# The additions of the MLPs' third group of block products to the residual, issued 200 places ahead in the scheduler's order

## The chip, the cores and the metric

The kernel runs as one program on one core of one Trainium2 chip. The metric is the device time of an execution in microseconds (us). Times inside an execution come from the hardware profiler and count from the first instruction.

The engines are named as in the profile: PE is the matrix engine (PEld its weight loads), DVE the vector engine, ACT the scalar engine, SP the queue that issues most loads. Each takes its instructions strictly in the order in which the program gives them to it, and an instruction that waits for another engine holds what stands behind it.

## The reference, cut to what matters

A trunk of two layers over 512 tokens of width 1024. Each layer has a token mixer, a layer norm, a squared-ReLU MLP of hidden width 4096, a second layer norm, and a gate.

```python
h = layer_norm(DEEPNORM_ALPHA * x + mix, ln_g[i, 0], ln_b[i, 0])
h = layer_norm(DEEPNORM_ALPHA * h + sq_relu_mlp(h, mlp_w1[i], mlp_w2[i]), ln_g[i, 1], ln_b[i, 1])
x = h + jax.nn.sigmoid(h @ ple_w_gate[i]) * (p[i] @ ple_w_proj[i])
...
def sq_relu_mlp(h, w1, w2):
    a = jax.nn.relu(h @ w1)
    return (a * a) @ w2
```

The change concerns the second matrix product of the MLP, `(a * a) @ w2`, and its sum with the residual. Both layers have it.

## The kernel before

**Precision.** Every matrix operand is split into a high part (`whi`, a rounded copy made by ACT at L114) and a low part (`wlo`, the rest, a subtraction by DVE at L116). A product is then three matmuls, high by high, high by low, low by high (`mm3`, L120 to L122). The operands that come from HBM are loaded as "units" of 128x1024: SP loads `raw` (L107), ACT makes `whi`, DVE makes `wlo`. There are three `raw` buffers, so a load waits until the split of the unit three before it has read its buffer.

**The MLP in groups.** The hidden width is cut into four groups of 1024. `hidden(g)` computes group g's activations; `half_blocks` (L355 on ACT, L356 to L364 on DVE) splits them in 2x2 blocks and forms sums of blocks. `block_product` multiplies one group with its part of `w2` in seven block products instead of eight (a Strassen scheme). `weight_sums` (L376 loads into `r`, L382 to L388 on DVE) forms the sums of weight blocks that this takes. A group's products run while the next group's activations are computed, in the order that the strings of `PERIODS` spell: T is a stretch of `hidden`, Q a product. The loop's index g is 1 for the first group's products and 3 for the third's, which run beside the activations of the fourth; the fourth group's products (g = 4) run alone, followed by the layer norm.

**A product.** Each has two halves of 128 tokens (c = 0 and 1), 12 matmuls each, into one PSUM bank each. Products named "x" use the two banks `py0` and `py1` and add up there one after another; "y" and "z" use two of the four `pj` banks. After each half, one DVE addition (L462, L466 or L468) adds the bank to the residual `acc`. The next product of the same banks may not write a bank before that addition has read it.

**The end of group 3 and the start of group 4.** Group 3 ends with its products p7 (banks `pj`), p5 (`py`), p4 (the same `pj`) and p3 (`py`), each with a pair of additions at L466. Group 4 has the order p1 (`py`), p7 (`pj`), p6 (`py`), p4, p5, p2, p3. p1 takes two raw units; p7 takes two sums of weights from `r`. Ahead of the fourth group the scheduler also places the gain of the next layer norm, a load into an `a` buffer (L195), which waits until `half_blocks` has read that buffer.

**What sets the order.** The kernel is traced in program order, and a scheduler puts the instructions of all engines in one order by priority, with buffers and banks given out on the way; each engine runs its own part of it. `tc.high_priority(offset=n)` moves what is traced inside n places ahead in that order. Constants: `SOON` is 40, `TURN` is 200, `LEAD` (units) is 100. In `block_product`, the additions of group 4 stood 40 places ahead, those of the groups 1 to 3 at their own place:

```python
with tc.high_priority(offset=SOON if after else 0):
```

Of the kernel before, what the change touches and what calls it, by code (L numbers as in the profile page):

```python
# [28 lines left out]
SOON = 40  # L29
TURN = 200  # L30

PERIODS = ("TTTTTTTT",) + 2 * ("TTQTQTQTQTQTQTQ",) + ("TTTQTQTQTQTQTQQ", "QQQQQQQ")
SUMS = (60, 300, 300, 300)
# [8 lines left out]
def trunk(ctx: ExitStack, tc, a):  # L42
# [21 lines left out]
    def mk(p, shape, tag, dt=F32, **kw):  # L64
        return p.tile(list(shape), dt, tag=tag, name=nm(tag), **kw)

    def f32(t):
        return t.bitcast(F32)
# [21 lines left out]
    def bank(p, tag):  # L90
        return mk(p, [P, T], tag)
# [8 lines left out]
    def behind(ins):  # L100
        return nullcontext() if ins is None else tc.issue_after(ins.ins)

    def unit(src, lead=LEAD):
        n = src.shape[1]
        with tc.high_priority(offset=lead):
            raw = mk(raws, [P, 1024], "raw")
            nc.sync.dma_start(raw[:, :n], src)  # L107
        return split(raw[:, :n], lead)

    def split(f, lead=LEAD):  # L110
        n = f.shape[1]
        with tc.high_priority(offset=lead):
            hi = mk(whip, [P, 1024], "whi", F32R)
            nc.scalar.copy(hi[:, :n], f)  # L114
            lo = mk(wlop, [P, 1024], "wlo", F32R)
            nc.vector.tensor_sub(lo[:, :n], f, f32(hi[:, :n]))  # L116
        return hi, lo

    def mm3(out, sh, sl, mh, ml, start, stop, **kw):
        nc.tensor.matmul(out, sh, mh, start=start, stop=False, **kw)  # L120
        nc.tensor.matmul(out, sh, ml, start=False, stop=False, **kw)  # L121
        marks["pe"] = nc.tensor.matmul(out, sl, mh, start=False, stop=stop, **kw)  # L122
# [36 lines left out]
    with tc.high_priority(offset=FIRST):  # L159
# [7 lines left out]
        for k in range(8):  # L167
            hi, lo = (v[:, k % 4, :] for v in early[k // 4])
            x, w = slots[k][:, 0:T], slots[k][:, T:768]
# [200 lines left out]
    def weight_sums(w, lead):  # L370

        t = [[None, None] for _ in range(4)]

        def load(i, u, src):
            t[i][u] = tmp("r", [P, 1024])
            nc.sync.dma_start(t[i][u], src)  # L376

        with tc.high_priority(offset=lead):
            for u in range(2):
                load(0, u, w[0][1][u])  # L380
                load(2, u, w[1][1][u])
                nc.vector.tensor_sub(t[2][u], t[2][u], t[0][u])  # L382
                load(1, u, w[0][0][u])
                nc.vector.tensor_sub(t[0][u], t[0][u], t[1][u])
                nc.vector.tensor_add(t[1][u], t[2][u], t[1][u])
            for u in range(2):
                load(3, u, w[1][0][u])
                nc.vector.tensor_sub(t[3][u], t[3][u], t[1][u])  # L388
        return t
# [44 lines left out]
            us.append((hi, lo))  # L434
        return us

    def block_product(w, blk, lead, first, after=None, sums=None):

        with behind(marks.pop(("turned", 0), None) if first else None):
            t1, t2, t3, t4 = weight_sums(w, lead)
        seen = set() if first else {(i, j) for i in range(2) for j in range(2)}
        banks = {}

        def product(x, f, name, start, i, j):
            us = [split(v) if f in (t1, t2, t3, t4) else unit(v) for v in f]
            if start:
                banks[name] = [bank(psy, "py%d" % c) if name == "x" else bank(psj, "pj") for c in range(2)]
            t = blk[x]  # L450
            for c in range(2):
                ps = banks[name][c]
                sl = slice(c * P, (c + 1) * P)
                for k in range(4):
                    hi, lo = us[k // 2]
                    ks = slice((k % 2) * 512, (k % 2 + 1) * 512)
                    w_ = hi[:, ks], lo[:, ks]
                    mm3(ps, t[:, 0, k, sl], t[:, 1, k, sl], *w_, start and k == 0, k == 3, skip_group_check=True)
                d = acc[:, 2 - 2 * i + c, j * 512 : (j + 1) * 512]
                with tc.high_priority(offset=SOON if after else 0):  # L460
                    if after and f in (w[1][0], t1, t4, w[1][1]):
                        marks["acc"] = nc.vector.tensor_tensor_reduce(  # L462
                            d, ps, d, 1.0, 0.0, ALU.add, ALU.add, sums[:, 2 - 2 * i + c, j : j + 1]
                        )
                    elif (i, j) in seen:
                        marks["acc"] = nc.vector.tensor_add(d, ps, d)  # L466
                    else:
                        marks["acc"] = nc.vector.scalar_tensor_tensor(d, d, ALPHA, ps, ALU.mult, ALU.add)  # L468
            seen.add((i, j))

        p1 = lambda: product("a11", w[0][0], "x", True, 0, 0)
        p2 = lambda: product("a12", w[1][0], "z", True, 0, 0)
        p6 = lambda: product("s2", t2, "x", False, 1, 0)
        p7 = lambda: product("s3", t3, "y", True, 1, 1)
        p5 = lambda: product("s1", t1, "x", False, 1, 1)
        p4 = lambda: product("a22", t4, "y", False, 1, 0)
        p3 = lambda: product("s4", w[1][1], "x", False, 0, 1)
        for f in (p1, p7, p6, p4, p5, p2, p3) if after else (p1, p2, p6, p7, p5, p4, p3):
            f()
            if after and f is p5:  # L480
                after(0), after(1)
            if after and f is p3:
                after(2), after(3)
            yield

    def mlp_and_gate(layer, h_s, last, turns=()):

        w1, w2 = a[f"w1_{layer}"], a[f"w2_{layer}"]
        blocks = {}
# [45 lines left out]
        for g, period in enumerate(PERIODS):  # L535
            if g < 4:
                tiles = hidden(g)
            if g > 0:
                if g == 4:
                    blk, after, turned, sums, later = norm_blocks(2 * layer + 1)  # L540
                    p_s = (mk(w4, [P, 2, T], "a", F32R), mk(w4, [P, 2, T], "b", F32R))
                    praw = mk(raws, [P, 1024], "raw")
                    nc.sync.dma_start(praw, a[f"pT_{layer}"].rearrange("p k t -> p (k t)"))
                    praw = praw.rearrange("p (k t) -> p k t", k=2)
                    nc.scalar.copy(p_s[0], praw)
                    nc.vector.tensor_sub(p_s[1], praw, f32(p_s[0]))
                w = [[[w2[8 * g - 8 + 4 * i + 2 * j + u] for u in range(2)] for j in range(2)] for i in range(2)]
                products = block_product(w, blocks.pop(g - 1), SUMS[g - 1], g == 1, *((after, sums) if g == 4 else ()))
            for n, op in enumerate(period):
                next(tiles if op == "T" else products)  # L550
                if 0 < g < 4 and (op == "Q" or n == 1):
                    next(ahead, None)
                if g == 4:
                    for _ in ahead:
                        pass
# [125 lines left out]
    first = [bank(psy, "py0"), bank(psy, "py1")]  # L681
# [313 lines left out]
    out_project(a["wso"][12:16], ys[3], False, *after, scale=rms_group(3, bank(psm, "pm")), spread=True)  # L995
    begin("mlp0")
    x_s, late = mlp_and_gate(0, h_s, False, [lambda c=c: after[1](c) for c in (2, 3)])
    begin("hgrn")

# [367 lines left out]
    out_project(a["who"][4:8], halves[1], False, *after)  # L1367
    begin("mlp1")
    mlp_and_gate(1, h_s, True)
    phase[1].__exit__(None, None, None)  # L1370

# [118 lines left out]
```

## Time and profile before

| | |
|---|---|
| median of 3 runs | 1407.03 us (1405.84 to 1407.28) |
| profiled execution | 1406.46 us, its span 1404.7 us |
| PE busy | 1397.1 us (99% of the span) |
| DVE busy | 1078.4 us (77%) |
| ACT busy | 775.8 us (55%) |
| granted TensorE clock | 1.000 |

The profiled execution is 1.8 us longer than its span, which lies ahead of the first instruction and after the last, and 0.6 us under the median of the runs. The groups' additions at L466 are 80 instructions of 0.68 us. A matmul of 512 columns is listed with 0.39 us, but the next one starts 0.227 us later: they overlap, so the distance between starts is what counts for PE.

### The profile page before, as it was taken

Reading aid. Unit: us, or ns where it says so; the run is one execution under the profiler, and the core shown is the slowest. Engines: PE = TensorE matmul, PEld = TensorE weight load, DVE = VectorE, ACT = ScalarE, POOL = GpSimd, SP = SyncE. Lnnn points to the kernel's source line nnn. Section 1 sums busy time; section 2 is a strip of 40 time slices with the busy share of each in tenths; the row PEclk is TensorE's granted clock in tenths of the full one; section 3 lists DMA queues with packets and bytes.
Section 4 is the critical chain, followed back from the end, with each engine's and each line's share of the span. In section 5 each row is a group of like instructions: output and inputs, shape, how many; then the busy total and the mean of one; then the engine's idle time right before and its main releaser. Section 6 shows DMA issues by size and latency. Waiting matters only on the chain.

```text
span 1404.7 us, 20463 instructions
## 1 busy us (share of the span) xinstructions
PE 1397.1 (99%) x7957; PEld 1167.6 (83%) x7957; DVE 1078.4 (77%) x1780; ACT 775.8 (55%) x1165; POOL 2.4 (0%) x11
## 2 busy tenths in 40 slices
PE   9999999999999999999999999999999999999998
PEld 7888888888988888887888888888898888888787
DVE  7998877696867879679885775776785787778886
ACT  7886666573554555455564446465455464544563
POOL 0000000000000000000000000000000000000000
PEclk9999999999999999999999999999999999999999
DMA  8424333323354764653473321222173656646264
GB/s 296 158 99 135 105 106 120 105 91 106 132 183 143 238 219 162 212 194 135 134 288 120 106 91 67 86 94 73 61 255 114 213 177 223 217 151 210 97 243 155
DMA packets 66817, 214.68 MB, mean 153 GB/s; under 512 B 7712, under 2 KB 8352, under 8 KB 66592
## 3 DMA queue, kind: packets, MB, share of 16 engines
q1 hardware_dynamic: 57504, 196.59, 41.1%
q10 hardware_dynamic: 9216, 16.78, 3.3%
q8 instruction: 62, 1.02, 0.3%
q14 instruction: 35, 0.29, 0.1%
HBM read 194.41 MB, written 18.94 MB: 152 GB/s over the span
## 4 chain that ended last, share of the span: by engine, by line
PE 90%; DVE 5%; DMA 2%; ACT 1%; issue 1%; DVEq 0%; ACTq 0%; SPq 0%
PE pj L120 23%; PE pj L122 23%; PE pj L121 23%; PE py L120 5%; PE py L121 5%; PE py L122 5%; DMA r<-in_w 2%; DVE wlo L116 2%; PE py L880 1%; PE py L1147 1%; PE py L882 1%; DVE b L356 1%; DMA raw<-in_w 1%; PE pt L863 0%; DVE acc L466 0%
## 5 line engine op out<-in xcount | busy, mean ns | idle before, releaser
L116 DVE TENSOR_TENSOR wlo<-raw,whi 128x1024 fp32r<-128x1024 f32 x222 | 269.5, 1221 | 170.6 <-ACT whi L114 169.0
L114 ACT CAST whi<-raw 128x1024 fp32r<-128x1024 f32 x222 | 232.7, 1050 | 288.2 <-PE pj L121 147.9
L120 PE MATMUL pj<-b,whi 128*128 128x512 f32 (+1 forms) x1000 | 379.6, 380 | 0.0
L121 PE MATMUL pj<-b,whi 128*128 128x512 f32 (+1 forms) x1000 | 377.3, 377 | 0.0
L122 PE MATMUL pj<-b,wlo 128*128 128x512 f32 (+1 forms) x1000 | 377.3, 377 | 0.0
L122 PEld LDWEIGHTS pj<-b,wlo 128*128 128x128 f32 x1000 | 188.2, 188 | 34.7
L121 PEld LDWEIGHTS pj<-b,whi 128*128 128x128 f32 x1000 | 188.2, 188 | 34.3
L120 PEld LDWEIGHTS pj<-b,whi 128*128 128x128 f32 x1000 | 187.9, 188 | 34.2
L122 PE MATMUL pj<-whi,b 128*128 128x512 f32 x530 | 206.0, 389 | 0.0
L120 PE MATMUL pj<-whi,b 128*128 128x512 f32 x496 | 196.1, 396 | 0.2 <-DVE cv L753 0.2
L121 PE MATMUL pj<-wlo,b 128*128 128x512 f32 x496 | 193.1, 390 | 0.0
L122 PEld LDWEIGHTS pj<-whi,b 128*128 128x128 f32 x530 | 99.5, 188 | 20.7 <-DVE b L1342 0.2
L114 ACT CAST whi<-r 128x1024 fp32r<-128x1024 f32 x64 | 67.2, 1053 | 88.3 <-PE pj L121 67.7
L120 PEld LDWEIGHTS pj<-whi,b 128*128 128x128 f32 x496 | 93.1, 188 | 20.7 <-issue 0.7
L121 PEld LDWEIGHTS pj<-wlo,b 128*128 128x128 f32 x496 | 93.2, 188 | 18.5
L120 PE MATMUL py<-whi,b 128*128 128x512 f32 x256 | 100.5, 393 | 2.2 <-DVE acc L466 2.2
L122 PE MATMUL py<-whi,b 128*128 128x512 f32 x256 | 99.7, 389 | 0.0
L121 PE MATMUL py<-wlo,b 128*128 128x512 f32 x256 | 99.6, 389 | 0.0
L116 DVE TENSOR_TENSOR wlo<-r,whi 128x1024 fp32r<-128x1024 f32 x64 | 77.7, 1219 | 27.6 <-ACT whi L114 26.8
L120 PEld LDWEIGHTS py<-whi,b 128*128 128x128 f32 x256 | 48.1, 188 | 12.8 <-DVE acc L466 3.0
L122 PEld LDWEIGHTS py<-whi,b 128*128 128x128 f32 x256 | 48.0, 188 | 10.1
L121 PEld LDWEIGHTS py<-wlo,b 128*128 128x128 f32 x256 | 48.1, 188 | 9.8
(375 smaller groups left out, 1934.4 us busy)
## 6 DMA issues: line engine op xcount, KB each, us to landing
raw<-in_w SPq DMA_DIRECT2D x112, 512.0 KB, 3.7
r<-in_w SPq DMA_DIRECT2D x64, 512.0 KB, 4.2
raw<-in_wssd SPq DMA_DIRECT2D x38, 512.0 KB, 3.9
a<-csd SPq DMA_DIRECT2D x16, 512.0 KB, 3.7
raw<-in_wso SPq DMA_DIRECT2D x16, 512.0 KB, 3.8
pre<-sg ACTq DMA_DIRECT2D x32, 256.0 KB, 4.8
whi<-pre SPq DMA_DIRECT2D x16, 512.0 KB, 5.4
wlo<-pre SPq DMA_DIRECT2D x16, 512.0 KB, 6.3
```

Of the source, the lines that this page charges most:

```text
L114: nc.scalar.copy(hi[:, :n], f)
L116: nc.vector.tensor_sub(lo[:, :n], f, f32(hi[:, :n]))
L120: nc.tensor.matmul(out, sh, mh, start=start, stop=False, **kw)
L121: nc.tensor.matmul(out, sh, ml, start=False, stop=False, **kw)
L122: marks["pe"] = nc.tensor.matmul(out, sl, mh, start=False, stop=stop, **kw)
L356: nc.vector.tensor_sub(lo, f, f32(hi))
L880: nc.tensor.matmul(yd[64 * r : 64 * r + 64, sl], xdt[:, c, r, :], m[:, r, sl], start=True, stop=c == 0)
L882: nc.tensor.matmul(yd[64 * r : 64 * r + 64, sl], pv[:, c - 1, r, :], ecs[:, r, (c - 1) * P : c * P], start=False, stop=True,)
L1147: nc.tensor.matmul(ps[r][32 * b : 32 * b + 32, base + n * c : base + n * c + n], kk[r][:, ts], moving(r, 4 * c + b), start=True, stop=True,)
```

## The change

`block_product` gets an argument `soon`, the offset for its additions. The call for g = 3 gives it TURN = 200, in both layers. Groups 1, 2 and 4 keep theirs.

```diff
-    def block_product(w, blk, lead, first, after=None, sums=None):
+    def block_product(w, blk, lead, first, after=None, sums=None, soon=0):
...
-                with tc.high_priority(offset=SOON if after else 0):
+                with tc.high_priority(offset=SOON if after else soon):
...
-                products = block_product(w, blocks.pop(g - 1), SUMS[g - 1], g == 1, *((after, sums) if g == 4 else ()))
+                products = block_product(w, blocks.pop(g - 1), SUMS[g - 1], g == 1, *((after, sums) if g == 4 else ()), soon=TURN if g == 3 else 0)
```

No instruction is added or removed. DVE, ACT, PE and SP each get the same instructions in another order near the end of group 3, in the same way in both layers; below is layer 0. A name ends in a number of its own: `py_850` and `py_851` are the banks of group 3's products p5 and p3, `pj_5343` and `pj_5344` those of its p7 and p4; `py_934` and `py_935` are those of group 4's p1, `pj_5650` and `pj_5651` those of its p7. `raw_5602` and `raw_5608` are p1's two units, `raw_5531` is the second unit of group 3's p3.

DVE, while PE computes group 3's p5 and the last activations; + is the order now, - the order before:

```order
 L356 TENSOR_TENSOR b_815_4952<-a_5225,b_815_4952 128x512
+L466 TENSOR_TENSOR acc_94<-py_850_5096,acc_94 128x512
 L388 TENSOR_TENSOR r_5596<-r_5596,r_5583 128x1024
-L466 TENSOR_TENSOR acc_94<-py_850_5096,acc_94 128x512
 L388 TENSOR_TENSOR r_5599<-r_5599,r_5592 128x1024
+L466 TENSOR_TENSOR acc_94<-py_851_5097,acc_94 128x512
+L356 TENSOR_TENSOR b_819_4956<-a_4959,b_819_4956 128x512
 L116 TENSOR_TENSOR wlo_5535<-raw_5531,whi_5533 128x1024
-L356 TENSOR_TENSOR b_819_4956<-a_4959,b_819_4956 128x512
 L116 TENSOR_TENSOR wlo_5606<-raw_5602,whi_5604 128x1024
-L466 TENSOR_TENSOR acc_94<-py_851_5097,acc_94 128x512
```

The additions of p5 stand earlier; the split of `raw_5531`, which frees a `raw` buffer, now stands behind the second of them and behind an L356 that it used to precede.

DVE, some five rows later, at the end of group 3:

```order
+L466 TENSOR_TENSOR acc_94<-pj_5344,acc_94 128x512
+L116 TENSOR_TENSOR wlo_5644<-r_5580,whi_5642 128x1024
+L116 TENSOR_TENSOR wlo_5648<-r_5589,whi_5646 128x1024
+L466 TENSOR_TENSOR acc_94<-py_850_5096,acc_94 128x512
 L360 TENSOR_TENSOR b_5373<-a_5225,b_5373 128x2x256
-L116 TENSOR_TENSOR wlo_5644<-r_5580,whi_5642 128x1024
 L362 TENSOR_TENSOR a_5225<-a_5225 128x2x256
-L116 TENSOR_TENSOR wlo_5648<-r_5589,whi_5646 128x1024
+L116 TENSOR_TENSOR wlo_5680<-r_5583,whi_5678 128x1024
+L356 TENSOR_TENSOR blk_4958<-b_5027,blk_4958 128x512
+L466 TENSOR_TENSOR acc_94<-py_851_5097,acc_94 128x512
```

The last three additions of group 3 (p4's second half and both of p3's) used to stand behind the whole of `half_blocks`' sums; now they stand among them, p3's second one behind four other operations. The five rows ahead of this piece, the same in both, are an L356, the split of `raw_5608` (L116), p4's first addition (L466) and two L356.

PE at the same place, before:

```order
L121 MATMUL py_851_5097<-wlo_5535,blk_4315 128x512
L122 MATMUL py_851_5097<-whi_5533,blk_4315 128x512
L120 MATMUL pj_5650<-whi_5642,blk_4957 128x512
L121 MATMUL pj_5650<-wlo_5644,blk_4957 128x512
L122 MATMUL pj_5650<-whi_5642,blk_4957 128x512
```

PE at the same place, now:

```order
L121 MATMUL py_851_5097<-wlo_5535,blk_4315 128x512
L122 MATMUL py_851_5097<-whi_5533,blk_4315 128x512
L120 MATMUL py_934_5614<-whi_5604,b_815_4952 128x512
L121 MATMUL py_934_5614<-wlo_5606,b_815_4952 128x512
L122 MATMUL py_934_5614<-whi_5604,b_815_4952 128x512
```

Before, group 3's p3 was followed by 23 of p7's 24 matmuls, then by p1; now p1, which writes the banks that p3 has just left, follows p3 directly, and p7 comes after it.

SP at the same place:

```order
 L376 DMA r_5599<-in_w_0 128x1024
 L107 DMA raw_5602<-in_w_0 128x1024
+L195 DMA a_5563<-in_ln 128x1024
 L107 DMA raw_5608<-in_w_0 128x1024
-L195 DMA a_5563<-in_ln 128x1024
 L107 DMA raw_5808<-in_w_0 128x1024
```

The load of the norm's gain now stands ahead of the load of p1's second unit. On ACT, the casts of the same stretch change places in step with DVE's rows.

## Prediction

> **What bounds the kernel now.** I read the page first (busy times, the chain that ended last, the costly groups), then PE's waits, then the stretch around each wait in order of time.
>
> ```profile
> PE 1397.1 (99%) x7957; PEld 1167.6 (83%) x7957; DVE 1078.4 (77%) x1780; ACT 775.8 (55%) x1165; POOL 2.4 (0%) x11
> PE 90%; DVE 5%; DMA 2%; ACT 1%; issue 1%; DVEq 0%; ACTq 0%; SPq 0%
> L120 PE MATMUL py<-whi,b 128*128 128x512 f32 x256 | 100.5, 393 | 2.2 <-DVE acc L466 2.2
> ```
>
> PE works through 99% of the span, so time is won only where PE stands still or by taking matmuls away, and the change takes none away. The 77% of DVE is a mean and says nothing on the ends of stages. The last row shows the one place in the MLPs where PE waits: 2.2 us on the additions that this change moves. PE's waits say the same:
>
> ```profile
> PE py L120 <- DVE acc L466: 2.2, 2, 1.1
> PE pm L155 <- DVE y L152: 1.1, 1, 1.1
> PE pj L120 <- DVE cv L753: 0.2, 1, 0.2
> ```
>
> Two waits, one a layer, are most of what all of PE's waits come to. PE in order of time shows what they are:
>
> ```profile
> 658.02 0.39 PE L120 MATMUL pj<-whi,blk 128*128 128x512 f32 x1
> ...
> 663.01 0.39 PE L121 MATMUL pj<-wlo,blk 128*128 128x512 f32 x1
> 664.46 0.50 PE L120 MATMUL py<-whi,b 128*128 128x512 f32 x1 [1.06 <-DVE acc L466]
> 664.80 0.40 PE L121 MATMUL py<-wlo,b 128*128 128x512 f32 x1
> ...
> 1314.70 0.50 PE L120 MATMUL py<-whi,b 128*128 128x512 f32 x1 [1.14 <-DVE acc L466]
> 1315.04 0.40 PE L121 MATMUL py<-wlo,b 128*128 128x512 f32 x1
> ```
>
> Starts are 0.227 us apart when nothing waits (22 steps from 658.02 to 663.01). From 663.01 the next should have started at 663.24; it started at 664.46, so 1.22 us are lost, and 0.11 us more since the first matmul after a wait takes 0.34 us to the second. In layer 1 the idle time is 0.08 us longer (1.14 against 1.06). Lost are 1.33 + 1.41 = 2.74 us: that is 0.19% of 1407 and the most that removed waits can bring. The first matmul that waits is p1 of group 4; it may write the bank only when group 3's p3 has been added. Why DVE is late:
>
> ```profile
> 642.21 1.23 DVE L388 TENSOR_TENSOR r<-r,r 128x1024 f32<-128x1024 f32 x1
> 643.35 1.22 DVE L116 TENSOR_TENSOR wlo<-raw,whi 128x1024 fp32r<-128x1024 f32 x1
> 644.49 0.69 DVE L356 TENSOR_TENSOR b<-a,b 128x512 fp32r<-128x512 f32 x1
> ...
> 649.71 1.23 DVE L116 TENSOR_TENSOR wlo<-raw,whi 128x1024 fp32r<-128x1024 f32 x1 [2.20 <-ACT whi L114]
> 650.85 0.68 DVE L466 TENSOR_TENSOR acc<-pj,acc 128x512 f32<-128x512 f32 x1
> 651.95 1.29 DVE L356 TENSOR_TENSOR b<-b,b 128x512 fp32r<-128x512 f32 x2 [0.42 <-ACT b L355]
> ...
> 661.98 0.68 DVE L466 TENSOR_TENSOR acc<-pj,acc 128x512 f32<-128x512 f32 x1
> 662.59 1.22 DVE L116 TENSOR_TENSOR wlo<-r,whi 128x1024 fp32r<-128x1024 f32 x1
> 663.72 1.28 DVE L466 TENSOR_TENSOR acc<-py,acc 128x512 f32<-128x512 f32 x2
> ```
>
> DVE stands still for 2.20 us until 649.71, waiting for the cast of p1's second unit, and then works without a pause worth the name until p3's additions at 663.72. An operation on 128x1024 holds DVE for 1.14 us (643.35 to 644.49), one on 128x512 for 0.60 us. The cast itself waited for a load, and that load for a buffer; the chain of work shows it in both layers:
>
> ```profile
> 644.60 3.93 DMA raw<-in_w
> 648.62 1.05 ACT whi L114
> ...
> 1287.71 5.00 DMA r<-in_w
> ...
> 1295.19 3.58 DMA raw<-in_w
> 1298.87 1.05 ACT whi L114
> ```
>
> The load was issued at 644.60, as the split that started at 643.35 ended (it reads the buffer), and took 3.93 us.
>
> **The change, part by part.** *Added and removed instructions:* none, 0 us. *The additions ahead of p3's:* PE waits for none of them before, and earlier ones release banks earlier: 0 for PE. They cost DVE its place, counted next.
>
> *DVE up to the load.* Before the split that frees the buffer, DVE now has done p7's second addition (0.60 us; it now stands ahead of the split that releases a buffer for the last `r` loads, so these and the second L388 come that much later, L388 at 642.81), then p5's second addition and the L356 that stood behind the split (1.20 us). The split starts at 642.81 + 1.14 + 1.20 = 645.15 and not 643.35: the load of p1's second unit is issued 1.80 us later, at 646.40. What hid that before, DVE's 2.20 us of idle time, is the time in which this load runs, so nothing hides it: the split of the unit, 5.11 us after the issue (644.60 to 649.71), starts at 651.51, if the load takes as long as before.
>
> *DVE from there to p3's additions.* In the order given above: split 1.14, p4's addition 0.60, two L356 1.20, p4's second addition 0.60, two splits 2.28. The L355 that the two L356 wait for follow the cast directly now, since ACT has done L523 and L525 ahead of it, so the wait of 0.42 us goes. Sum 5.82: p3's first addition starts at 657.33, and ends 0.68 us later at 658.01. Then its own slot and L360, L362 (1.80), a split 1.14, an L356 0.60: p3's second addition starts at 660.87 and ends at 661.55.
>
> *PE.* p1 now stands where p7's first matmul stood, at 658.02. Until a matmul starts, 0.06 us pass after the addition's end (663.72 + 0.68 = 664.40 to 664.46). So p1's first half waits some 0.05 us. Its second half is due 12 x 0.227 = 2.72 us later, at 660.74, and starts at 661.61: a wait of 0.87 us, 0.98 with the restart. The 5.2 us of p7 that covered p3's additions before lie behind p1 now, and the two effects nearly cancel: 1.33 lost becomes 0.98, a gain of 0.35 us a layer. Layer 1 has the same orders and a wait of the same kind; I take 0.35 there too. Together -0.70 us.
>
> *p7, p6 and what follows on PE.* p7 starts at about 664.5 instead of 658.0; its operands (the splits of its `r` units, right ahead of p3's first addition, and an L356 on `blk` two rows behind the second, which ends at 660.87 + 0.60 + 0.60 + 0.68 = 662.75) are ready 1.7 us ahead, and a late load moves both sides alike. p6 starts after 48 matmuls, at the same place as before. 0 us. *ACT:* casts of the same units in another order, covered by its 45% of idle time; on the way to the end only the one counted.
>
> *SP.* The norm's gain is loaded ahead of the unit, and not behind it:
>
> ```profile
> 637.68 0.33 SPq L376 DMA_DIRECT2D r<-in_w  x1
> 645.20 0.33 SPq L195 DMA_DIRECT2D a<-in_ln  x1
> 667.89 0.33 SPq L107 DMA_DIRECT2D raw<-in_w  x1
> ```
>
> The first of two `r` loads that end in DVE's L388, as the chain has it, L388 itself, and the time from issue to landing of the four L195:
>
> ```profile
> 636.59 3.68 DMA r<-in_w
> ...
> 640.36 1.23 DVE L388 TENSOR_TENSOR r<-r,r 128x1024 f32<-128x1024 f32 x1 [0.38 <-DMA r<-in_w]
> ...
> DMA to landing us min/median/max: 3.7/4.1/5.8
> ```
>
> The gain's load (L195) waits for the L356 that started at 644.49, so it is issued as that ends. This L356 now stands just ahead of the split that frees the `raw` buffer. So the unit's load is issued one split, 1.14 us, behind another load of 512 KB. No row of before has this pair in this order. Bounds: it may cost nothing (the load takes 3.93 and 3.58 us in the two layers, as before), or the unit may take as long as the slowest L195, 5.8 us, which was issued 0.60 us behind the unit's load (644.60 to 645.20). The nearest rows are two `r` loads 1.09 us apart: the first, from 636.59, took 3.68 us; DVE, which waits for both at L388, started 4.53 us after the second was issued (637.68 to 642.21), some 4.44 us of it the load (the first had 0.09 us from landing, 640.27, to DVE's start at 640.36). Layer 1's second load of that pair took 5.00 us. I take 4.44 for both layers: 0.51 and 0.86 us later, and each passes to PE undiminished, since p1 has nothing to spare: +1.37 us. The ends are 0 and (5.8 - 3.93) + (5.8 - 3.58) = 4.09 us.
>
> A later unit's load (667.89) waits for L546 on DVE, which ran at 666.65 and now stands further back:
>
> ```profile
> 666.65 1.22 DVE L546 TENSOR_TENSOR b<-raw,a 128x1024 fp32r<-128x1024 f32 x1
> 680.02 1.05 ACT L114 CAST whi<-raw 128x1024 fp32r<-128x1024 f32 x1 [3.02 <-PE pj L122]
> ```
>
> From p3's second addition at 660.87 there are ten operations of 0.60 and five of 1.14 us ahead of L546, which so starts at 672.6, 5.9 us later. The load then is issued at 673.8 and lands, at 4.4 us, by 678.2; its cast did not start before 680.02, held by PE. 0 us, with 1.8 us of cover.
>
> The Trainium skill speaks against so high a price for the unit's load: DMA: Bandwidth & Descriptors, "Anatomy of one DMA", gives a fit (measured on the GpSimd path) of about 2.0 us fixed plus the bytes at 436 GB/s. By it 512 KB move in 1.2 us, a load 1.14 us behind another would be held by some 0.06 us, and the sum would be -0.6 us. The rows above, 3.68 against 4.44 us, do not agree with it.
>
> *Sum:* -0.70 + 1.37 = +0.67 us. The profiled execution of 1406.46 us becomes 1407.1; from the median of the runs, 0.57 us higher, 1407.7.
>
> **The rivals.**
>
> *1. The load is hardly delayed.* That is the lower end of the SP term. For it: the L195 load is issued while no other load is in flight. Against it: the `r` rows. -0.70 us: 1406.3. The fit that the Trainium skill gives in DMA: Bandwidth & Descriptors would bring this case about.
>
> *2. The waits go altogether*: DVE reaches p3's additions 0.9 us earlier than my sum. For it: most slots come from back-to-back rows, and a faster landing by that much would do it. Against it: the load is issued 1.80 us later for certain if DVE's order holds. -2.74 us: 1404.3.
>
> *3. Slower: p1 waits for its second unit's load in earnest.* One mechanism: the unit's load, now second in the queue, lands late; ACT and DVE stand behind it in order, and every us of it arrives at PE, which no longer has p7 in front as cover. If it takes 5.8 us in both layers the sum is -0.70 + 4.09 = +3.39: 1410.4. It decides (0.2%, 2.8 us) when the two loads together are 3.5 us later than before. For it: that 5.8 was seen in this very stretch; against: with fewer loads ahead of it than L195 had then.
>
> **How the numbers follow.** 0.2% or 2.8 us is about what a measurement of this kernel can tell from no change. The forecast (the wait changes its place and the load is somewhat late, between -0.1 and +2.5 us) gets 0.55, rival 1 gets 0.25, rival 2 gets 0.07, rival 3 gets 0.10, anything else 0.03. Rivals 1 and 2 stay inside 0.2% by their own numbers (2.74 is 0.195%); noise may carry rival 2 over it, so faster gets 0.03, slower 0.10, same 0.87. The range leaves out rival 2's end and most of rival 3: from 1405.2 (rival 1 less a spread of the runs of about 1 us) to 1409.6 (the forecast with both loads 1 us later still).
>
> **What would show it.** After the change PE should still wait for L466, in each layer at both halves of p1: at the first by what the load is late, 0.5 to 0.9 us, and 12 matmuls later at the second by 0.8 to 0.9 us. p1's second unit should be issued about 1.8 us later against PE's place than now, 1.14 us behind L195, and take about 4.4 us. PE's busy time and its clock stay. A wait at the second half alone speaks for rival 1, none at either for rival 2, one of 1.8 us or more at the first half for rival 3. The prediction is wrong if PE waits elsewhere in the two stretches, at p7 above all, or if p1's second unit is issued where it was, which would mean that DVE's rows ahead of it wait less than I count.

## The result, and the profile after

| | median | lowest to highest | against before (95% interval) |
|---|---|---|---|
| before | 1406.11 us | 1405.56 to 1407.28 | |
| after | 1410.94 us | 1410.43 to 1412.26 | 1.0034 [1.0022, 1.0046] |

The change makes the kernel slower, by 4.8 us. The prediction was 1407.7 us, within 1405.2 to 1409.6: it is wrong. The profiled execution of after took 1412.26 us, its span 1410.5 us; that is 5.8 us over the profiled execution of before, and it was the slowest of the runs shown.

The row of the page, and two of PE's waits, that answer to those of before:

```profile
L120 PE MATMUL py<-whi,b 128*128 128x512 f32 x256 | 101.2, 395 | 6.1 <-DVE acc L466 6.1
```

```profile
PE py L120 <- DVE acc L466: 6.1, 3, 3.0
...
PE py L120 <- ACT whi L174: 0.4, 1, 0.4
```

The wait on the additions is where it was expected, but has 6.1 us and not 2.2; no other wait came up in the two stretches. PE in order of time, p3's last matmul and p1's first ones, in layer 0 and then in layer 1:

```profile
658.22 0.39 PE L122 MATMUL py<-whi,blk 128*128 128x512 f32 x1
661.63 0.76 PE L120 MATMUL py<-whi,b 128*128 128x512 f32 x1 [3.03 <-DVE acc L466]
662.20 0.63 PE L121 MATMUL py<-wlo,b 128*128 128x512 f32 x1
...
664.64 0.40 PE L121 MATMUL py<-wlo,b 128*128 128x512 f32 x1
...
1311.63 0.39 PE L122 MATMUL py<-whi,blk 128*128 128x512 f32 x1
1314.49 0.47 PE L120 MATMUL py<-whi,b 128*128 128x512 f32 x1 [2.47 <-DVE acc L466]
...
1318.07 0.50 PE L120 MATMUL py<-whi,b 128*128 128x512 f32 x1 [0.57 <-DVE acc L466]
```

In layer 0 p1 was due 0.227 us after 658.22, at 658.45, and started at 661.63: 3.18 us are lost. Then seven steps, to 664.64, take 3.01 us instead of 1.59: 1.42 us more, because the clock is lowered. The same stretch by windows (the number after POOL is the granted clock):

```profile
661.00:662.50 1.50, 0.87 (x2) 0.80 (x3) 1.47 (x3) 0.38 (x1) 0.00 (x0) 0.52 0.00 0
662.50:664.50 2.00, 2.00 (x6) 1.52 (x6) 2.00 (x4) 2.00 (x4) 0.00 (x0) 0.50 0.00 0
```

The lowered clock did not cost all of these 1.42 us. p1's second half started at 665.78. At the full clock it would have been due at about 664.5, but p3's second addition (664.47, in the next fence) lets it start only 0.68 + 0.06 us later, at 665.21, and with the 0.11 us of a restart that is some 0.5 us sooner than it came. So the clock's own share is about 0.5 us, an estimate from these rows; the rest of the 1.42 us took the place of the wait at the second half, which layer 1 shows.

In layer 1 p1 was due at 1311.86 and started at 1314.49, 2.63 us lost; its second half started 3.58 us after its first instead of 2.72, 0.86 us lost. The clock stayed. Together 4.60 + 3.49 = 8.1 us against 2.74 before: 5.4 of the 5.8 us. The wait at L174 (0.4 us, at the start of the program) is most of the rest.

Why the additions are late: DVE in the stretch before them. The load of p1's second unit, as the chain of work has it (time, duration), stands in the second fence.

```profile
644.66 1.23 DVE L388 TENSOR_TENSOR r<-r,r 128x1024 f32<-128x1024 f32 x1 [0.70 <-DMA r<-in_w]
...
647.00 2.35 DVE L116 TENSOR_TENSOR wlo<-raw,whi 128x1024 fp32r<-128x1024 f32 x2
...
654.99 1.22 DVE L116 TENSOR_TENSOR wlo<-raw,whi 128x1024 fp32r<-128x1024 f32 x1 [5.03 <-ACT whi L114]
...
660.80 0.68 DVE L466 TENSOR_TENSOR acc<-py,acc 128x512 f32<-128x512 f32 x1
...
664.47 0.68 DVE L466 TENSOR_TENSOR acc<-py,acc 128x512 f32<-128x512 f32 x1
```

```profile
648.25 5.58 DMA raw<-in_w
...
1301.61 5.08 DMA raw<-in_w
```

PE reached the end of p3 at 658.45 here and at 658.02 before, so 0.43 us are taken off a difference of times below ("against PE"). L388's second instance then is 2.45 - 0.43 = 2.02 us later than before; p1's second unit is issued 3.65 - 0.43 = 3.22 us later (648.25 against 644.60), its load takes 1.65 us longer (5.58 against 3.93; 1.50 in layer 1), and its split starts 5.28 - 0.43 = 4.85 us later. DVE waits 5.03 us for it, not 2.20. From that split on the order is as I counted it: p3's first addition 5.81 us behind the split (predicted 5.82), its second 3.67 us behind the first (predicted 3.54).

In layer 1 the same steps give less: L388 starts 1298.02 - 1292.80 = 5.22 us later than before, 3.68 of which PE is later too (1311.86 against 1308.18), so 1.54 us against PE.

So the question is what made L388 2.02 us late, when I had counted 0.60. Further up, DVE shows it; the stretch that the section on the change prints begins behind these rows, and the order of DVE differs from before here already. Before, at a split and at the next operation that waits for a load:

```profile
620.13 1.22 DVE L116 TENSOR_TENSOR wlo<-raw,whi 128x1024 fp32r<-128x1024 f32 x1
...
629.55 1.23 DVE L382 TENSOR_TENSOR r<-r,r 128x1024 f32<-128x1024 f32 x1 [1.88 <-DMA r<-in_w]
```

SP's issue of the load that this split allows, in before, and the `r` load behind it, from the chain of before (its time, its length):

```profile
621.38 0.33 SPq L107 DMA_DIRECT2D raw<-in_w  x1
```

```profile
624.31 5.16 DMA r<-in_w
```

After, DVE and SP at the same places:

```profile
618.17 0.69 DVE L466 TENSOR_TENSOR acc<-py,acc 128x512 f32<-128x512 f32 x1
...
621.16 0.68 DVE L466 TENSOR_TENSOR acc<-py,acc 128x512 f32<-128x512 f32 x1
621.76 0.68 DVE L356 TENSOR_TENSOR b<-b,b 128x512 fp32r<-128x512 f32 x1
622.36 1.22 DVE L116 TENSOR_TENSOR wlo<-raw,whi 128x1024 fp32r<-128x1024 f32 x1
...
631.84 1.23 DVE L382 TENSOR_TENSOR r<-r,r 128x1024 f32<-128x1024 f32 x1 [2.42 <-DMA r<-in_w]
```

```profile
623.64 0.33 SPq L107 DMA_DIRECT2D raw<-in_w  x1
625.35 3.10 SPq L376 DMA_DIRECT2D r<-in_w  x2
```

The two additions of p6 (618.17 and 621.16) and an L356 now stand ahead of this split. It frees the `raw` buffer for the second unit of p3, some 20 us ahead of the stretch that I had studied. That unit's load is issued 2.26 - 0.43 = 1.83 us later against PE, so the `r` load follows it by 1.71 us and no longer by 2.93. The `r` load itself is issued 1.04 - 0.43 = 0.61 us later against PE, and now takes 6.4 us from issue to landing; DVE's L382, which waits for it, starts 2.29 - 0.43 = 1.86 us later against PE.

DVE's next split is held by something else as well. ACT's cast for it waits until a store of gate weights (L423, issued by ACT's queue) has landed, and the chain of after runs over these stores in both layers, not over the `r` load. ACT's cast and DVE's split in before:

```profile
630.20 1.05 ACT L114 CAST whi<-raw 128x1024 fp32r<-128x1024 f32 x1 [2.20 <-DMA pre<-whi]
```

```profile
631.30 1.21 DVE L116 TENSOR_TENSOR wlo<-raw,whi 128x1024 fp32r<-128x1024 f32 x1
```

The store, cast and split in after, and the store in layer 1, from the chain:

```profile
626.06 0.33 ACTq L423 DMA_DIRECT2D pre<-whi  x1
...
632.03 1.05 ACT L114 CAST whi<-raw 128x1024 fp32r<-128x1024 f32 x1 [3.61 <-DMA pre<-wlo]
```

```profile
633.11 1.23 DVE L116 TENSOR_TENSOR wlo<-raw,whi 128x1024 fp32r<-128x1024 f32 x1
```

```profile
1279.48 5.73 DMA pre<-whi
```

The view names `pre<-wlo`, but that store lands only at 632.9; the one of `whi` lands at 631.96, 0.07 us ahead of the cast. The two stores are issued where they were against PE (625.64 and 627.00 before, 626.06 and 627.41 now), but take 5.9 and 5.5 us to land, where it was 4.5 and 3.8. Either wait alone would have held the split until about 633 (L382 at 631.84 and its 1.14 us; the cast at 632.03 and its 1.05 us). The split is 1.81 - 0.43 = 1.38 us later against PE. Behind it stands p7's second addition, whose 0.60 us I had counted: 1.38 + 0.60 = 1.98 of L388's 2.02 us. So some 1.4 us, the part that I had not counted, come from one load and two stores that land late together.

### The profile page after: what moved, and what is told of

Read it like the earlier page. It is cut to its first block, busy times and chain, and to the rows that moved or that the text cites. A ratio compares the mean times of both kernels' runs of the same rounds, so it can differ in the third digit from the quotient of the medians.

```text
span 1410.5 us, 20463 instructions
## 1 busy us (share of the span) xinstructions
PE 1398.6 (99%) x7957; PEld 1168.7 (83%) x7957; DVE 1078.7 (76%) x1780; ACT 775.1 (55%) x1165; POOL 2.4 (0%) x11
## 4 chain that ended last, share of the span: by engine, by line
PE 93%; DVE 3%; DMA 3%; ACT 1%; issue 1%; SPq 0%; ACTq 0%; DVEq 0%
PE pj L120 24%; PE pj L121 23%; PE pj L122 23%; PE py L120 5%; PE py L121 5%; PE py L122 5%; DVE wlo L116 1%; PE py L880 1%; PE py L1147 1%; DMA raw<-in_w 1%; PE py L882 1%; DMA r<-in_w 1%; PE pt L863 0%; DMA acc<-in_xw 0%; DVE acc L466 0%
## 5 line engine op out<-in xcount | busy, mean ns | idle before, releaser
L116 DVE TENSOR_TENSOR wlo<-raw,whi 128x1024 fp32r<-128x1024 f32 x222 | 269.6, 1222 | 176.1 <-ACT whi L114 174.9
L116 DVE TENSOR_TENSOR wlo<-r,whi 128x1024 fp32r<-128x1024 f32 x64 | 77.5, 1220 | 25.6 <-ACT whi L114 24.8
```

## The experiments

Theories at the start. A: DVE's rows ahead of splits make the loads late, p1's second unit above all. B: PE has lost its cover, since p1 follows p3 directly and p7 comes behind it. C: the gain's load (L195) ahead of the unit's makes that load slow. All edits are against after.

**p3's additions alone ahead.**

```diff
-                with tc.high_priority(offset=SOON if after else soon):
+                with tc.high_priority(offset=SOON if after else soon if f is w[1][1] else 0):
```

> Only the additions of group 3's last product p3 stand 200 places ahead; those of its other six products keep the place that they had before the change. PE's order is that of the changed kernel (p1 right behind p3), SP's order is that of before. Theory A (the loss comes from additions ahead of DVE's splits, which free the load buffers, so that p1's second unit lands late): the unit's load is issued where it was before, PE waits at neither half of p1, and 2.3 to 2.7 us are won against before (about 1403.6 us). Theory B (the loss comes from PE's order: p7's 23 matmuls no longer cover p3's additions): PE still waits 2 to 3 us a layer at p1 and the time is 1409 to 1411 us. Theory C (the loss comes from the norm's gain loaded ahead of the unit): no loss here either, since SP's order is the old one; the run doesn't tell A from C.

Measured: 1404.67 us, ratio 0.9987 [0.9978, 0.9996]. PE waits for no L466 at all; the longest row of its waits, 1.1 us on L152 at the start of the program, is one that before has too. That is 1.7 us less than its own runs of before (1406.38), not the 2.3 to 2.7 expected. SP's loads and DVE's splits up to p1's second unit have the order of before here, while p1 follows p3 directly on PE as in after. DVE's two additions of p3 and the PE rows that they release (p1's two halves):

```profile
656.81 0.69 DVE L466 TENSOR_TENSOR acc<-py,acc 128x512 f32<-128x512 f32 x1
659.21 0.69 DVE L466 TENSOR_TENSOR acc<-py,acc 128x512 f32<-128x512 f32 x1
```

```profile
658.14 0.39 PE L120 MATMUL py<-whi,b 128*128 128x512 f32 x1
...
660.86 0.39 PE L120 MATMUL py<-whi,b 128*128 128x512 f32 x1
```

Each addition ends about 0.6 to 1.0 us ahead of its matmul (656.81 + 0.69 and 658.14; 659.21 + 0.69 and 660.86). The place of p1 on PE alone costs nothing: B falls as a cause by itself. This version is faster than both kernels.

**The others ahead, p4's and p3's at their old place.**

```diff
+                with tc.high_priority(offset=SOON if after else 0 if f is w[1][1] or f is t4 else soon):
```

> The reverse of the first: the additions of p1, p2, p6, p7 and p5 of group 3 stand 200 places ahead, those of p4 and p3 keep their old place. SP has the changed kernel's order (the gain's load ahead of p1's second unit). Theory A: the unit lands 4 to 5 us late as in the changed kernel, DVE reaches p3's additions that much later, with all of the sums of the activations' blocks still ahead of them, and PE waits 5 to 6 us a layer: 1413 to 1418 us. Theory B (lost cover alone): no loss, 1405 to 1407 us. Theory C: between, 1408 to 1411 us, with the unit's load issued where it was and only its landing late.

Measured: 1418.21 us, ratio 1.0084 [1.0070, 1.0098], the slowest of all, although p7 stands ahead of p1 on PE as before:

```profile
PE py L120 <- DVE acc L466: 7.3, 2, 3.7
```

p7 is not a clean cover here: its own matmuls wait 2.4 us in the two layers for blocks that ACT and DVE make (L355, L356). The clock falls at both waits too (last section). The additions of p1, p2, p6, p7 and p5, for which PE never waited, together do the harm, and p3's do the good; which of the five pairs it is, this run doesn't tell.

**The norm's parameters loaded at its first chunk.** The gain and bias leave this stretch; nothing is computed otherwise.

```diff
-        gb = ln_params(i)
+        gb = []
...
         def chunk(c):
+            gb or gb.extend(ln_params(i))
```

> The changed kernel with the norm's gain and bias loaded only when the first chunk is normalised, so no other load stands right ahead of p1's second unit. Theory A with the price that the trace gives (the unit's load takes 5.6 and 5.1 us behind the gain's, against 3.9 and 3.6 before): the load is issued as late as in the changed kernel but takes 3.6 to 4 us, PE's wait shrinks by 1.5 us a layer, the clock is not lowered in layer 0, and 4 to 5 us of the 4.8 come back: 1406 to 1408 us. Theory C (the gain's load is all of the loss): 1404.5 us or less, with no wait left. Theory B: as slow as the changed kernel, 1410 to 1411 us.

Measured: 1407.69 us, ratio 1.0008 [0.9998, 1.0017]. Beside the 1406.38 us of its own runs of before that is +1.3: 3.5 of the 4.8 us come back. The chain of this run has the unit's load at 3.71 and 3.79 us, as fast as before the change, in place of 5.58 and 5.08:

```profile
647.50 3.71 DMA raw<-in_w
...
1298.30 3.79 DMA raw<-in_w
```

PE still waits on L466, four times and 3.1 us in all:

```profile
PE py L120 <- DVE acc L466: 3.1, 4, 0.9
```

C is real as a part: 5.58 - 3.71 and 5.08 - 3.79 make 3.2 us for both layers, and with the 0.5 us of the clock they come near the 3.5 us. As the whole loss C falls, since PE still waits. The 4 to 5 us that theory A expected back did not come.

**Small stores.** The last eight stores of transformed weights in each layer (L416, L423) write 16 columns of 512, and the loads that read them read another block; so part of the weights is not the reference's.

```diff
-                            nc.scalar.dma_start(to, x)
+                            nc.scalar.dma_start(to[:, : 512 if (u, h) != (1, 1) else 16], x[:, : 512 if (u, h) != (1, 1) else 16])
```

(L416 likewise.)

> The changed kernel in which the last eight stores of prepared gate weights in each layer (ACT's queue, 256 KB each, in the stretch of group 3) store 16 columns of 512; the gate then takes its second half of weights from the first half's stores, so the output is not the reference's. Theory A with loads colliding with stores: the weight load behind DVE's first late L382 takes 5 us or less (6.4 in the changed kernel, 5.2 before), ACT's cast of the unit behind those stores starts 1.4 us earlier, so everything down to p1's second unit comes 1.4 us earlier: PE waits 1.3 to 1.8 us a layer instead of 2.5 to 3.1, the clock stays, and the time is 1406 to 1408 us. If the stores don't matter (the lateness is all DVE's own order): 1410 to 1411 us.

Measured: 1408.75 us, ratio 1.0014 [1.0005, 1.0023], a little above what was expected: +2.4 us against its own runs of before, so 2.4 of the 4.8 come back. The `r` load takes 3.8 us in this run, 6.4 in after, and DVE's L382 finds it landed (no wait is listed):

```profile
628.87 1.22 DVE L382 TENSOR_TENSOR r<-r,r 128x1024 f32<-128x1024 f32 x1
```

ACT's queue issues such stores beside that load, in after the one at 626.06 shown above. So the traffic of the stores is part of what makes the late loads slow. The run changes two things at once, though: the cast that waits for these stores is free earlier too (it starts at 628.92 and waits 0.32 us), so it doesn't tell the `r` load's share from the cast's. The profiled execution was the fastest of its runs, so its waits on L466 (1.9 us in all) are those of a faster run than the median; where the rest of the median's time lies isn't settled.

**p6's additions alone ahead.** By now the rows further up were read, and A was split: A1 holds p6's additions to be the missing part, A2 p5's and the gain's load alone.

```diff
+                with tc.high_priority(offset=SOON if after else soon if f is t2 else 0):
```

> Of group 3's additions only p6's two are issued 200 places ahead; PE and SP have the order of before, DVE differs from before in some ten rows some 25 us ahead of the end of group 3. Upstream theory (A1: p6's additions ahead of the split that frees p3's second raw buffer make that load some 1.8 us late, it then runs together with an r load and two stores, and the whole of DVE up to p1's second unit is some 2 us late): p1's second unit is issued 1.5 to 2.0 us later against PE than before, DVE reaches p3's additions as much later, and since PE has used up p7 as cover before, its two waits of 1.1 us grow to 2.6 to 3.1 us each: 1409.0 to 1410.5 us. Rival (A2: the lateness comes only from p5's additions right ahead of the split and from the gain's load ahead of the unit, p6's additions change nothing that matters): waits as before, 1405.6 to 1406.9 us.

Measured: 1410.51 us, ratio 1.0032 [1.0019, 1.0044]. Two additions some 40 us ahead of p1, for which PE does not wait, make a loss of 4.1 us by themselves, 0.7 us less than the whole change. The profiled execution is the fastest of the five, 1409.22 us, 2.8 us over that of before, and its clock is 1.000; two slower ones, 1412.15 and 1412.45 us, have mean clocks of 0.999 and 0.997. PE and SP have the order of before, and the two waits of before have grown from 1.06 and 1.14 us:

```profile
665.68 0.50 PE L120 MATMUL py<-whi,b 128*128 128x512 f32 x1 [2.61 <-DVE acc L466]
...
1317.54 0.50 PE L120 MATMUL py<-whi,b 128*128 128x512 f32 x1 [2.69 <-DVE acc L466]
```

The upstream rows are those of after again: on SP the load of p3's second unit (622.96) 1.70 us ahead of the `r` load (624.66), which takes 6.3 us, and ACT's two stores, which take 4.9 to 5.8 us. p1's second unit is issued at 646.05 in the chain of this run and lands in 3.70 us, as it did before; only its issue is late, by 1.8 us:

```profile
646.05 3.70 DMA raw<-in_w
```

**All but p6's.**

```diff
+                with tc.high_priority(offset=SOON if after else soon if f is not t2 else 0):
```

> The change without p6's two additions; PE and SP keep the order of the changed kernel, and DVE the same rows ahead of the split that frees the buffer. Upstream theory (A1): p3's second raw unit and the r loads come as in before, p1's second unit is issued 1.2 to 1.8 us later against PE than before instead of 3.2, the wait at p1's first half falls from 3.0 and 2.5 us to 1.0 to 1.7, no lowered clock: 1406.8 to 1408.6 us. Rival (A2): waits and time stay those of the changed kernel, 1410 to 1411.5 us.

Measured: 1407.15 us, ratio 1.0008 [0.9999, 1.0017], 0.7 us over before, which the interval doesn't tell from no change. The wait at p1's second half is there in both layers and that at its first half in one, 2.0 us in all; at the first half 1.0 to 1.7 us in each layer had been expected, and 0 and 0.8 came. The chain has the slow load behind L195 in layer 1:

```profile
1295.25 5.48 DMA raw<-in_w
```

```profile
PE py L120 <- DVE acc L466: 2.0, 3, 0.8
```

A1 holds, A2 falls: without p6's additions most of the loss is gone, with the gain's load still ahead of the unit. But one step of A1 does not hold. On SP the `r` load is as close behind the load of p3's second unit here as in after:

```profile
621.94 0.33 SPq L107 DMA_DIRECT2D raw<-in_w  x1
623.67 4.05 SPq L376 DMA_DIRECT2D r<-in_w  x2
```

It lands in 4.3 us all the same, and the two stores of ACT in 2.6 to 3.2 us. They are issued 1.81 and 3.03 us behind the `r` load here (625.48 and 626.70), 0.71 and 2.06 us behind it in after. So the nearness of the two loads is not by itself what makes the `r` load slow. That p6's additions move it against the stores fits all these runs, and the run with small stores above, but no run moves this distance alone.

**The change, with p7 ahead of p1 in group 4.**

```diff
-        for f in (p1, p7, p6, p4, p5, p2, p3) if after else (p1, p2, p6, p7, p5, p4, p3):
+        for f in (p7, p1, p6, p4, p5, p2, p3) if after else (p1, p2, p6, p7, p5, p4, p3):
```

> The change, and group 4 takes p7 ahead of p1, so that PE has p7's 24 matmuls (5.4 us) between p3 and p1 again, with DVE's additions in the changed order. Theory A (p1's second unit and the additions behind it are late by some 3.2 us, and nothing else is wrong): the cover hides most of it, the waits on L466 sum to under 2 us, no lowered clock: 1404.5 to 1407.0 us. Rival B2 (the split that brings p7's operands stands behind the late unit as well, so p7 waits instead of p1): waits of over 2 us in each layer at p7's first matmuls or at p1, 1409 us or more.

Measured: 1404.19 us, ratio 0.9984 [0.9975, 0.9993], faster than both kernels and about as fast as p3's additions alone, with no wait on L466 left. The time is 0.3 us under what theory A expected, and the cover is not the only reason. p3's second unit is loaded as late as in after (623.37, with p3's end on PE at 658.17, against 623.64 and 658.45); the `r` load behind it takes 5.0 us, not 6.4, and p1's second unit is split at 654.40. DVE in this run:

```profile
647.03 1.22 DVE L116 TENSOR_TENSOR wlo<-r,whi 128x1024 fp32r<-128x1024 f32 x1
...
648.76 1.22 DVE L116 TENSOR_TENSOR wlo<-r,whi 128x1024 fp32r<-128x1024 f32 x1
...
654.40 1.22 DVE L116 TENSOR_TENSOR wlo<-raw,whi 128x1024 fp32r<-128x1024 f32 x1
...
656.14 0.69 DVE L466 TENSOR_TENSOR acc<-py,acc 128x512 f32<-128x512 f32 x1
...
658.54 0.69 DVE L466 TENSOR_TENSOR acc<-py,acc 128x512 f32<-128x512 f32 x1
```

Against PE's end of p3 the unit lands 1.8 us earlier than in after (issued at 647.14, 4.6 us), but its split starts only 0.3 us earlier. DVE no longer stands still in front of it. It does the splits of p7's operands (647.03 and 648.76), L356's and an addition of p4 there, which in after stood behind the late unit (its two splits of `r` at 658.54). So p3's first addition comes 1.7 us behind the unit's split and not 5.8. The second ends at 659.23, and p1's second half, if p1 followed p3 directly on PE, would be due at 658.17 + 2.72 = 660.89: by these rows no wait would be left in layer 0 even without p7 in front, and none either if the split came 0.3 us later, as in after. That is worked out, not run: no run has this order of DVE with p1 directly behind p3. B2 falls, since PE waits nowhere for p7. What made the late unit so dear in after is the ready work that stood behind it on DVE.

The lateness in layer 0, from the traces: the issue of p1's second unit against PE, later than before, and its time from issue to landing:

| kernel | median us | unit issued later | lands in |
|---|---|---|---|
| before | 1406.11 | 0 | 3.93 |
| after | 1410.94 | 3.2 | 5.58 |
| p3 alone | 1404.67 | -0.2 | 3.60 |
| p6 alone | 1410.51 | 1.8 | 3.70 |
| all but p6 | 1407.15 | 0.9 | 4.77 |

The 1.8 and the 0.9 us come to 2.7 of the 3.2.

## Why the prediction was wrong, step by step

- **The additions ahead of p3's "cost DVE its place, counted next": the step that failed.** I counted p7's second addition and p5's, and left out p6's two, which stand ahead of a split too. I had followed the order only from p7's additions on, not at every split that frees a buffer. The term of 0.60 us for L388 measured 2.02 in layer 0 and 1.54 in layer 1: p7's 0.60 was right, and what p6's rows set off, a load and two stores that land late, came on top. The sum had no term for that, nor for ACT's cast, which waits for the stores. p6 alone costs 4.1 us (1410.51 against the 1406.42 of its own runs of before); the change without it costs 0.7 us, and my sum, which had no p6, was +0.67. That these meet is partly chance: there the unit is issued 0.9 us late in layer 0, not 1.8, as its `r` load landed faster than before (4.3 us against 5.2), and its own load then takes longer than I had it (4.77 and 5.48 against 4.44).
- **What was missing in the sum, in us:** L388 1.42 and 0.94, the unit's load 1.14 and 0.64, the clock about 0.5. Together 4.6, and with the forecast's +0.67 that is 5.3; the rows of PE gave 5.4.
- **p5's addition and the L356, 1.20 us:** right, 3.22 - 2.02 = 1.20.
- **The load behind L195, 4.44 us:** too small; 5.58 and 5.08 in after, 4.77 and 5.48 without p6's additions. Against before, after's are 1.65 and 1.50 us more, and not 0.51 and 0.86. Inside the ends I gave (up to 5.8 us), but I took the row of the two `r` loads, which was too fast a neighbour. The fit from the Trainium skill (DMA: Bandwidth & Descriptors, "Anatomy of one DMA"), by which I estimated that a load 1.14 us behind another would be held by some 0.06 us, does not describe these loads, which SP issues: they were held by 1.65 and 1.50 us.
- **DVE from the split to p3's additions, 5.82 us, and the second half's wait, 0.87 us:** right; 5.81 us in layer 0 and, for the wait, 0.86 us in layer 1. In layer 0 the lowered clock filled the time of that wait.
- **p7, the later unit and all else at 0 us:** right; no further wait came. That the lost cover of p7 is made up by earlier additions was right as well: with p3's additions alone ahead PE had neither the cover nor a wait.
- **"PE's clock stays":** wrong in layer 0 of the profiled execution, 1.42 us on the first half and about 0.5 us in the end. It was no accident of that execution: the mean clock is 0.998 in five of the seven of after, the profiled one among them, and 0.999 in the other two, where the profiled execution of before has 1.000 and the runs of before beside the experiments 1.000 or 0.999.
- **Rival 3** gave the right sign and, at 1410.4 us, nearly the right time, and its mark (a wait of 1.8 us or more at p1's first half) came. Its mechanism holds for one part: with the gain's load moved away 3.5 us came back, and p6's additions alone cost 4.1. These two are not parts of one sum, since the second was measured with before's order of PE. That the time came so near is partly luck: the two loads were 3.2 us later than before, not 4.09, and the late L388, which rival 3 did not have, made up the rest.
- **The ends of the range** are each about 0.1 us off their own working: 1406.3 less 1 is 1405.3, and 1407.7 plus 2 is 1409.7. The result lies beyond both values of the upper end.

## What to carry to other kernels

An instruction moved ahead on an in-order engine is paid by whatever stood there: list every row that it passes, back to where it now stands, and mark the rows that free a buffer for a load, since the transfers that moved here met others and landed later still. Move only what somebody waits for: of the two pairs of additions that were moved alone, p3's paid and p6's cost. Where an operation must wait for a late load, look at what stands behind it on its engine: a unit issued 2.4 us late (647.14, p3's end at 658.17) cost nothing once the ready splits and additions stood ahead of it.

## What the hardware showed beyond that

**The clock.** In layer 0 of after the granted clock fell to 0.5 in an idle time of PE of 3.03 us, for about 3.4 us: by the windows shown, 0.52 from 661.00 to 662.50 and 0.50 to 664.50. After idle times of 2.47, 2.61 and 2.69 us, in the rows above, it stayed: in layer 1 of after p1's first half took no longer than its 2.72 us and the wait behind it, and the execution with p6's additions alone has a mean clock of 1.000. That is no bound either: in another execution of that same kernel, 1412.45 us, the mean clock is 0.997, and waits and clock inside it are not recorded. In the second experiment it fell with both waits of 3.7 us:

```profile
670.30:673.70 3.40, 3.40 (x10) 2.66 (x9) 2.58 (x4) 0.00 (x0) 0.00 (x0) 0.50 0.00 0
...
1325.00:1326.20 1.20, 0.00 (x0) 0.00 (x0) 1.20 (x3) 0.00 (x0) 0.00 (x0) 0.77 0.00 0
1326.20:1332.40 6.20, 6.14 (x14) 4.79 (x15) 4.08 (x7) 0.00 (x0) 0.00 (x0) 0.50 0.26 82
```

In layer 0 PE was at work again from 669.47, and the lowered stretch of 3.4 us lies behind that; in layer 1 it began inside the wait (none of PE's work in the window at 0.77) and lasted over 6 us. The Trainium skill's TensorE: Matmul & The Clock Gate ("What's actually happening") describes a window of some 3.4 us that runs on its own; these lengths and the shifting begin agree with it. Its rule of no idle gaps over some 3.4 us ("HAM oscillation — how this bites in real kernels") is not a safe bound here: 3.03 us were enough.

**Transfers in company.** p1's second unit, 512 KB, landed in 3.6 to 3.9 us without the gain's load ahead of it and in 4.5 to 5.6 us when issued 1.14 us behind it. For the `r` load the store behind it goes with its time better than the load ahead of it (layer 0):

| kernel | load ahead by | first store behind by | `r` load lands in |
|---|---|---|---|
| all but p6 | 1.73 | 1.81 | 4.3 |
| before | 2.93 | 1.33 | 5.2 |
| after | 1.71 | 0.71 | 6.4 |
| p6 alone | 1.70 | 0.66 | 6.3 |
| p7 ahead of p1 | 1.70 | 0.72 | 5.0 |
| small stores | 1.69 | 0.72 | 3.8 |

The row of p7 ahead of p1 has the distances of after and 5.0 us, so these distances alone don't set the time.
